# Two-layer trunk of attentions: the first head's loads on another queue, four projection tiles in another order, and another layout of on-chip memory for the second attention

## The chip, the cores and the metric

The kernel runs on one core of a Trainium2 chip. The metric is the device time of one execution in microseconds (us). One core has TensorE (matrix products, written to PSUM), VectorE, ScalarE and GpSimd, and SyncE, which here only starts DMAs. The engines run their own programs in order and wait for each other by semaphores. DMAs are started from the queues of SyncE, ScalarE and GpSimd and are carried out by 16 DMA engines that the core has for all of them. In the profile PE is TensorE, PEld its weight loads, DVE VectorE, ACT ScalarE, POOL GpSimd, SP SyncE; SPq, ACTq and POOLq are the starting of DMAs and other work of the sequencers.

## The reference

2048 tokens of width 1024 go through two layers, each `x <- LayerNorm(alpha * x + mixer(x))`. The mixer of layer 0 is a causal attention with forget gates (FoX), that of layer 1 a sparse attention (DSA): a small indexer selects 256 keys for each query, and only these count in the softmax. Both have 8 heads of 128 and a gate in front of the output weights.

```python
def _fox_mixer(x, w_in, b_f, w_out):
    q, k, v, f_logit, gate = _split(x @ w_in, [H * dh, H * dh, H * dh, H, D])
    cum = jnp.cumsum(jax.nn.log_sigmoid(f_logit + b_f), axis=1)
    ...
        s = einsum('bqhd,bshd->bhqs', q_b, k) * scale + c_b - cum_t
        s = where(kpos <= qpos, s, -inf)
        return einsum('bhqs,bshd->bqhd', softmax(s), v)
    ...
    return (silu(gate) * o) @ w_out

def _dsa_mixer(x, ..., w_in, kv_norm_g, w_uk, w_uv, w_out):
    q, ckv, kr, qi, ki, wi, gate = _split(x @ w_in, [H * dh, dc, dr, HI * di, di, HI, D])
    ...
        isc = einsum('bqhs,bqh->bqs', relu(einsum('bqhd,bsd->bqhs', qi_b, ki) * di ** -0.5), wi_b)
        isc = where(kpos <= qpos, isc, -inf)
        _, idx = lax.top_k(isc, k_sel)
        logits = einsum('bqhc,bqkc->bhqk', qf_b, kv_lat[idx]) * dh ** -0.5
        o_lat = einsum('bhqk,bqkc->bqhc', softmax(logits), sel[..., :dc])
    ...
    return (silu(gate) * o) @ w_out
```

## The kernel before, in words

Every operand is split into a high and a low half-precision part, and a product is three matmuls (`mm3`, lines 319 to 321: high by high, high by low, low by high). The split is a copy on ScalarE (line 328) and a subtraction (line 325) on GpSimd or VectorE.

The trunk runs one stage after the other: the projections of layer 0 (`fox_proj`), `attention(0)`, `out_proj(0)`, the projections of layer 1 (`dsa_jobs`, in three lists `first`, `second` and `rest`; the index scores and the selection run between them on VectorE and GpSimd and end in masks that GpSimd stores to DRAM, line 1647), `attention(1)`, `out_proj(1)`. Between stages K, V, q and the gates lie in DRAM tensors (`scr_k1`, `scr_kr` and `scr_kn`, `scr_v1`, `scr_v2`, `scr_q1`, ...).

`attention(layer)` goes through 8 heads and for each through four chunks of 512 queries, in the order `ORD[layer]`: (2, 3, 1, 0) in layer 0, (1, 0, 3, 2) in layer 1. For 128 queries `qk_tile` forms scores in PSUM, VectorE evacuates them with the mask or bias added and takes the minimum (line 1054, into a room PR), ScalarE takes the exponential and its sum (line 1068) and copies the high part (line 1076), GpSimd subtracts the low part (line 325, into PP), and a transposing DMA of SyncE turns the pair (line 1081) into one of the rooms PT, PU and PX, which are taken in turn (`TURNED`). In long chunks one row of each pair is turned on TensorE instead (line 1088). `pv_tile` multiplies with V. `gate` (line 1019 on) takes the reciprocal of the four sums and multiplies it into the gate; `pv_end` (line 1126) multiplies the result with it and stores it.

`load_kv` loads K and V of a head, `load_chunk` a chunk's q, `gate` the gate, `load_masks` the masks. All are issued by SyncE, save those of K and V of the first head (h = 0), which ScalarE issues. Loads of the next head are issued in between (`jobs`).

On-chip memory is a sequence of phases. `PHASE` says how many rooms of each tag a phase has, `SIZE` their bytes, `ORDER` the order in which they lie behind each other. Rooms of the next phase lie over those of the phase before, and an instruction that first writes a room waits for the last uses of all that lies under it. Phase 0 are the eight rooms `KV` of X1, the split output of layer 0, which the projections of layer 1 read; two of them (g = 0, 1) hold one chunk of 512 tokens. Phase 2 are the rooms of the second attention. Phase 5 are eight rooms P of the split output weights (`load_wo`, line 1153), taken by the pairs of `WOP`.

The instructions' order on each engine is made from the program by a scheduler that simulates a timeline; so a changed layout or queue moves others' places, too.

Of the kernel before, what the change touches and what calls it, by code (L numbers as in the profile page):

```python
# [15 lines left out]
F16 = mybir.dt.float16  # L16
# [33 lines left out]
         {"K": 4, "V": 2, "PT": 1, "PU": 1, "PX": 1, "PR": 4, "PP": 3, "M": 1, "N": 3}, {"P": 8},  # L50
         {"A": 3, "X": 15}, {"P": 8}, {})
ORDER = ((), ("N", "I", "PR", "PT", "pad1", "PU", "K", "PP", "V", "PX"),
         ("N", "M", "PX", "PR", "K", "V", "PP", "pad2", "PT", "PU"), ("pad3", "P"), ("A", "X"), (),
         ("st", "GB", "u", "GA", "GC", "spare"))
SIZE = {"K": 2048, "V": 4096, "PT": 8192, "PU": 8192, "PX": 8192, "PR": 4096, "PP": 4096, "I": 128, "N": 256,
        "M": 2432, "pad1": 3200, "pad2": 896, "pad3": 4096, "P": 4096, "A": 4096, "X": 4096, "st": 4096,
        "u": 3584, "spare": 4096, "GA": 8448, "GB": 10752, "GC": 7936}
TURNED = ("PT", "PU", "PX")

PS_BUFS = {"S": 3, "T": 2, "U": 2, "O": 1}  # L60
UTAGS = "SUSUS"
# [5 lines left out]
ORD = ((2, 3, 1, 0), (1, 0, 3, 2))  # L67
# [10 lines left out]
FTAGS = "STUSTUS"  # L78
SCAN = 2

WOP = (((0, 1), (2, 3), (4, 5), (6, 7)), ((3, 4), (2, 5), (6, 7), (1, 0)))
OGS = (0, 1, 2, 3), (0, 1, 1, 1)
OGE = 3
AHEAD = 13
# [135 lines left out]
def weave(main, side, start, end):  # L220

    at = []
    for k, (jobs, lo, hi) in enumerate(((main, 0.0, 1.0), (side, start, end))):
        total, done = sum(c for c, _ in jobs), 0.0
        for i, (c, job) in enumerate(jobs):
            at.append((lo + (hi - lo) * (done + 0.5 * c) / total, k, i, (c, job)))
            done += c
    return [x[3] for x in sorted(at, key=lambda x: x[:3])]


class Trunk:
# [736 lines left out]
    def load_kv(self, layer, h):  # L968
        nc = self.nc
        st = {"layer": layer}  # L970

        rooms = FIRSTK[layer] if h == 0 else (("K", 1024), ("K", 1024))
        st["k"] = []

        def key(s):
            while sum(n for _, n in rooms[:len(st["k"])]) < s + 1024:
                tag, n = rooms[len(st["k"])]
                a = sum(n for _, n in rooms[:len(st["k"])])
                to = self.t(tag, [128, 2, n], F16)
                for rows, name, r in ((slice(0, 32), "kr", 0), (slice(32, 128), "kn", h * 96)) if layer else (  # L980
                        (slice(0, 128), "k1", h * 128),):
                    (nc.sync if h else nc.scalar).dma_start(
                        to[rows], self.scr[name][r:r + rows.stop - rows.start, :, a:a + n])
                st["k"].append(to)
                for b in range(a, a + n, 512):
                    st[b] = to[:, :, b - a:b - a + 512]

        def value(s):
            if s == 0:
                st["v"] = self.t("V", [128, NT, 2, 128], F16)  # L990
            t = s // 128
            v = self.scr["v2" if layer else "v1"][h]
            (nc.sync if h else nc.scalar).dma_start(st["v"][:, t:t + 8], v[:, t:t + 8])

        return st, [partial(f, s) for f in (key, value) for s in range(0, S, 1024)]

    def load_chunk(self, layer, h, c):
        nc = self.nc
        cs = {"layer": layer, "h": h, "c": c, "l": self.sums[:, c, 4 * h:4 * h + 4], "halves": []}
        q, parts = self.pair(("SC" if layer else "RW") if (h, c) == (0, ORD[layer][0]) else "E")  # L1000
        nc.sync.dma_start(q, self.scr["q2" if layer else "q1"][c, h * 128:(h + 1) * 128])
        cs["q"] = parts
        if layer:
            return cs
        if self.rel[0] != h:
            self.rel = h, [self.t("W", [128, 1024]) for _ in range(2)]
            for a, t in enumerate(self.rel[1]):
                nc.sync.dma_start(t, self.scr["rel"][h:h + 1, a * 1024:a * 1024 + 1024].to_broadcast([128, 1024]))
        cs["rel"] = self.rel[1]
        return cs  # L1010
# [15 lines left out]
    def qk_tile(self, cs, j, i):  # L1026

        nc = self.nc
        c = cs["c"]
        qt = 4 * c + j  # L1030
# [29 lines left out]
        if i == 0:  # L1060
            yield "turn"
            self.half_i += 1
            turned = self.t(TURNED[self.half_i % len(TURNED)], [128, 4 * qt + 6, 128], F16)
            cs["halves"].append({"cs": cs, "half": j // 2, "T": turned})
        up = self.tiny(1)
        per, neg = (self.scale(x, cs["layer"]) for x in ("per", "neg"))
# [2 lines left out]
        turned = cs["halves"][-1]["T"]  # L1069
# [8 lines left out]
        if c >= MERGE:  # L1078
            turned = turned[:, 2 * qt:]
# [185 lines left out]
    def dsa_jobs(self):  # L1265

        nc, A = self.nc, self.A
# [141 lines left out]
        def jobs(order):  # L1409

            out = []
            for m, ch in order:
                if m not in kept:
                    kept[:] = kept[-KEPT:] + [m]
                    out.append((0.0, partial(load, m)))
                else:
                    kept[:] = [x for x in kept if x != m] + [m]
                out.append((5.2, partial(tile, m, ch)))
            return out
# [3 lines left out]
        def over(tiles, *chunks):  # L1423
            return [(m, ch) for ch in chunks for m in tiles]
# [10 lines left out]
                ups.append((0.0, partial(at, ch + 1)))  # L1435
            ups += [(0.7, partial(up_value, ch, j, s)) for j in range(4) for s in range(2)]
        rest = []
        for m in range(6, 22):
            rest += jobs(over((m,), 0, 1, 2, 3))
        return first, second, weave(weave(rest, ups, *UPS), [(1.0, up)], UPL, UPL)  # L1440


# [231 lines left out]
```

## Time and profile before

| | us |
|---|---|
| median of three runs | 2780.16 |
| the runs | 2783.97, 2780.16, 2772.90 |
| the profiled execution | 2781.16 |
| its span in the trace | 2779.4 |
| TensorE busy | 2517.8 (91%) |
| VectorE busy | 1888.0 (68%) |
| ScalarE busy | 1419.7 (51%) |
| GpSimd busy | 858.8 (31%) |

Mean granted clock of TensorE is 0.968 of its full speed. A busy share is a mean over all stages. The rows further down give a start in us from the start of the span, a duration, the engine, the line of the kernel, the operation with output and input tiles, and in brackets how long the engine was idle before and on what it waited.

### The profile page before, as it was taken

What the parts mean: (1) busy time and instruction counts of PE and PEld (TensorE: products, weight loads), DVE (VectorE), ACT (ScalarE), POOL (GpSimd) and SP (SyncE); (2) the same over time, 40 slices, a digit from 0 to 9 for tenths busy, and PEclk for the clock granted to TensorE, in tenths of its full rate; (3) what the DMA queues carried; (4) which work ended last, traced back from release to release, by engine and by line L of the source; (5) the groups of instructions that cost most, each with busy time, mean ns of one, the idle gap of its engine ahead of it and who ended that gap; (6) DMA issues with size and microseconds to landing.
All of it is one profiled execution on the core that took longest, in us unless ns stands there. A gap on an engine that the chain in (4) does not pass through costs nothing. (4 is left out here: it accounts for less than half of the span.)

```text
span 2779.4 us, 44011 instructions
## 1 busy us (share of the span) xinstructions
PE 2517.8 (91%) x15919; PEld 1636.5 (59%) x15919; DVE 1888.0 (68%) x4662; ACT 1419.7 (51%) x2283; POOL 858.8 (31%) x601
## 2 busy tenths in 40 slices
PE   8788989999988889889999989899978888888898
PEld 7688534444665666668845444444435666666687
DVE  4786655444766666667748899888955666666565
ACT  6464343322665666632326876774535666666310
POOL 3465643330333334442210211110013333333421
PEclk9899999999999999999999999999989999999999
DMA  7456645214988888864332432222678888777642
GB/s 263 162 187 204 211 126 173 76 65 151 210 204 171 184 188 181 165 198 141 124 97 61 123 90 64 69 75 82 197 217 190 192 178 184 173 163 151 183 144 88
DMA packets 583809, 424.20 MB, mean 153 GB/s; under 512 B 398048, under 2 KB 473584, under 8 KB 583584
## 3 DMA queue, kind: packets, MB, share of 16 engines
q1 hardware_dynamic: 580544, 412.78, 56.2%
q10 hardware_dynamic: 1984, 4.20, 0.5%
q0 software_dynamic: 1056, 4.36, 0.4%
q8 instruction: 125, 2.05, 0.3%
q14 instruction: 100, 0.82, 0.1%
HBM read 219.88 MB, written 109.08 MB: 118 GB/s over the span
## 5 line engine op out<-in xcount | busy, mean ns | idle before, releaser
L325 POOL TENSOR_TENSOR PP<-PR,PP 128x640 f16<-128x640 f32 (+3 forms) x192 | 375.8, 1971 | 697.0 <-ACT PP L1076 525.5
L1068 ACT ACTIVATE PR<-PR,ty,small 128x1152 f32<-128x1152 f32 (+15 forms) x256 | 330.1, 1290 | 249.5 <-DVE ty L1067 245.5
L325 POOL TENSOR_TENSOR W<-RW,W 128x512 fp32r<-128x512 f32 (+1 forms) x124 | 160.0, 1310 | 540.7 <-ACT W L328 469.5
L325 POOL TENSOR_TENSOR W<-A,W 128x512 f16<-128x512 f32 x114 | 136.5, 1218 | 228.8 <-ACT W L328 192.2
L320 PEld LDWEIGHTS <-W 128*128 128x128 f16 x1184 | 116.3, 98 | 147.1 <-issue 13.9
L321 PEld LDWEIGHTS <-W 128*128 128x128 f16 x1184 | 116.3, 98 | 137.9 <-issue 2.9
L319 PEld LDWEIGHTS <-W 128*128 128x128 f16 x1184 | 116.6, 98 | 137.3 <-issue 3.2
L1076 ACT ACTIVATE PP<-PR 128x640 f16<-128x640 f32 (+3 forms) x192 | 186.2, 980 | 18.0 <-DMA PX<-PP 7.5
L320 PEld LDWEIGHTS <-V 128*128 128x128 f16 x1152 | 117.0, 102 | 104.4 <-issue 81.8
L319 PE MATMUL T<-KV,W 128*128 128x512 f16 x464 | 176.9, 381 | 0.4 <-DVE E L1250 0.4
L320 PE MATMUL T<-KV,W 128*128 128x512 f16 x464 | 177.1, 382 | 0.0
L321 PE MATMUL T<-KV,W 128*128 128x512 f16 x464 | 176.9, 381 | 0.0
L328 ACT ACTIVATE W<-RW 128x512 fp32r<-128x512 f32 (+1 forms) x124 | 73.4, 629 | 181.6 <-PE U L320 93.6
L1054 DVE CUSTOM_DVE_ANT_0 PR<-S,W,ty 128x512 f32<-128x512 f32 (+3 forms) x209 | 138.8, 664 | 38.0 <-PE S L1049 18.1
L319 PEld LDWEIGHTS <-V 128*128 128x128 f16 x1152 | 116.9, 101 | 64.0 <-DMA PX<-PP 17.0
L319 PE MATMUL S<-K,E 128*128 128x512 f16 (+3 forms) x379 | 132.3, 349 | 11.5 <-DVE ty L1054 10.7
L378 ACT ACTIVATE SC<-E,tz 128x512 f16<-128x512 f32 (+1 forms) x78 | 50.8, 682 | 172.5 <-DVE E L540 102.6
L320 PE MATMUL S<-K,E 128*128 128x512 f16 (+3 forms) x379 | 132.3, 349 | 0.0
L321 PE MATMUL S<-K,E 128*128 128x512 f16 (+3 forms) x379 | 131.9, 348 | 0.0
L1480 ACT ACTIVATE SC<-S,small 128x512 f32<-128x512 f32 (+2 forms) x182 | 111.8, 635 | 35.4 <-DVE GC L1485 7.1
L321 PEld LDWEIGHTS <-V 128*128 128x128 f16 x1152 | 117.2, 102 | 20.1 <-issue 0.8
L1088 PE MATMUL T<-ident,PR 128*128 128x128 f32 x768 | 116.6, 277 | 3.4 <-DVE PU L325 1.7
(503 smaller groups left out, 7836.0 us busy)
## 6 DMA issues: line engine op xcount, KB each, us to landing
A<-in_fw SPq DMA_DIRECT2D x38, 512.0 KB
QS<-in_fw SPq DMA_DIRECT2D x32, 512.0 KB
E<-scr_g SPq DMA_DIRECT2D x64, 256.0 KB
scr_og<-SC SPq DMA_DIRECT2D x64, 256.0 KB
RW<-scr_og SPq DMA_DIRECT2D x64, 256.0 KB
E<-scr_q SPq DMA_DIRECT2D x62, 256.0 KB
V<-scr_v SPq DMA_DIRECT2D x28, 512.0 KB
scr_g<-E SPq DMA_DIRECT2D x48, 256.0 KB
```

Source lines behind the costliest of these rows:

```text
L319: first = mm(o, lh, rh, start=start, stop=False, skip_group_check=True)
L320: mm(o, lh, rl, start=False, stop=False, skip_group_check=True)
L321: mm(o, ll, rh, start=False, stop=stop, skip_group_check=True)
L325: eng.tensor_tensor(out=o, in0=a, in1=b, op=OP.subtract)
L328: self.nc.scalar.activation(hi, src, AF.Copy)
L378: nc.scalar.activation(out[0], src, AF.Copy, scale=scale)
L1054: nc.vector.tensor_tensor_reduce(out=row[:, lo:hi], in0=sc[:, lo - a:hi - a], in1=bias, op0=OP.add, op1=OP.min, scale=-1.0, scalar=3e38 if ...
L1068: nc.scalar.activation(row, row, AF.Exp, bias=up, scale=neg, accum_out=cs["l"][:, j:j + 1])
L1076: nc.scalar.activation(hi, row, AF.Copy)
L1088: nc.tensor.transpose(ps[:, (k - a) * 128:(k - a + 1) * 128], row[:, k * 128:(k + 1) * 128], self.ident)
L1480: nc.scalar.activation(t, ps[:, :w], AF.Relu, scale=self.scales[:, 24:25])
```

## The change

There are four parts. The loads of K and V of the first head, in both attentions, go from ScalarE's queue to GpSimd's, and the very first q from SyncE's to GpSimd's. The last four projection tiles of layer 1 (18 to 21, gate columns) are made chunk by chunk, in the order 2, 3, 1, 0, and no longer tile by tile. In the second attention the rooms lie in another order, and the turned rooms are taken in another rotation. The eight rooms of the output weights of layer 1 are paired otherwise.

```diff
 ORDER = ((), ("N", "I", "PR", "PT", "pad1", "PU", "K", "PP", "V", "PX"),
-         ("N", "M", "PX", "PR", "K", "V", "PP", "pad2", "PT", "PU"), ("pad3", "P"), ("A", "X"), (),
+         ("N", "PR", "K", "PX", "V", "PP", "PT", "PU", "M", "pad2"), ("pad3", "P"), ("A", "X"), (),
...
-TURNED = ("PT", "PU", "PX")
+TURNED = ("PT", "PU", "PX"), ("PU", "PX", "PT")
...
-WOP = (((0, 1), (2, 3), (4, 5), (6, 7)), ((3, 4), (2, 5), (6, 7), (1, 0)))
+WOP = (((0, 1), (2, 3), (4, 5), (6, 7)), ((4, 3), (0, 1), (2, 5), (7, 6)))
...
-                    (nc.sync if h else nc.scalar).dma_start(
+                    (nc.sync if h else nc.gpsimd).dma_start(
                         to[rows], self.scr[name][r:r + rows.stop - rows.start, :, a:a + n])
...
-            (nc.sync if h else nc.scalar).dma_start(st["v"][:, t:t + 8], v[:, t:t + 8])
+            (nc.sync if h else nc.gpsimd).dma_start(st["v"][:, t:t + 8], v[:, t:t + 8])
...
-        nc.sync.dma_start(q, self.scr["q2" if layer else "q1"][c, h * 128:(h + 1) * 128])
+        eng = nc.gpsimd if (h, c) == (0, ORD[layer][0]) else nc.sync
+        eng.dma_start(q, self.scr["q2" if layer else "q1"][c, h * 128:(h + 1) * 128])
...
-            turned = self.t(TURNED[self.half_i % len(TURNED)], [128, 4 * qt + 6, 128], F16)
+            turned = self.t(TURNED[cs["layer"]][self.half_i % 3], [128, 4 * qt + 6, 128], F16)
...
-        for m in range(6, 22):
+        for m in range(6, 18):
             rest += jobs(over((m,), 0, 1, 2, 3))
+        rest += jobs(over((18, 19, 20, 21), *ORD[0]))
```

**ScalarE at the start of the second attention.** Before, from the projection's last evacuation (line 371) to the second exponential. V and K are rooms of the first head (a name's number is that of the tile), `kr` and `kn` the two parts of K.

```order
1493 L371 ACTIVATE E_23336<-O_23311,small 128x512
1494 L1632 UNCONDITIONAL_BRANCH
1495 L993 DMA V_24193<-scr_v_69 128x2048
1496 L982 DMA K_24213<-scr_kr 32x2x1024
1497 L1068 ACT_TABLE_LOAD
1498 L1068 ACTIVATE PR_24173,N_24152<-PR_24173,ty_24188,small 128x640
1499 L982 DMA K_24213<-scr_kn 96x2x1024
1500 L993 DMA V_24193<-scr_v_69 128x2048
1501 L1076 ACTIVATE PP_24174<-PR_24173 128x5x128
1502 L1068 ACTIVATE PR_24173,N_24152<-PR_24173,ty_24207,small 128x768
```

With the change, the same stretch on to the fourth exponential:

```order
1486 L371 ACTIVATE E_23336<-O_23311,small 128x512
1487 L1634 UNCONDITIONAL_BRANCH
1488 L1069 ACT_TABLE_LOAD
1489 L1069 ACTIVATE PR_24173,N_24152<-PR_24173,ty_24188,small 128x640
1490 L1077 ACTIVATE PP_24174<-PR_24173 128x5x128
1491 L1069 ACTIVATE PR_24173,N_24152<-PR_24173,ty_24207,small 128x768
1492 L1077 ACTIVATE PP_24174<-PR_24173 128x6x128
1493 L1069 ACTIVATE PR_24218,N_24152<-PR_24218,ty_24233,small 128x896
1494 L1077 ACTIVATE PP_24219<-PR_24218 128x7x128
1495 L1069 ACTIVATE PR_24218,N_24152<-PR_24218,ty_24251,small 128x1024
```

The four DMAs are gone from ScalarE. On GpSimd they now stand between the last mask store and the first split of the attention:

```order
428 L1649 DMA scr_mask<-GA_19190 128x1920
429 L1649 DMA scr_mask<-GA_19190 128x2048
430 L993 DMA V_24193<-scr_v_69 128x2048
431 L982 DMA K_24213<-scr_kr 32x2x1024
432 L982 DMA K_24213<-scr_kn 96x2x1024
433 L993 DMA V_24193<-scr_v_69 128x2048
434 L325 TENSOR_TENSOR PP_24174<-PR_24173,PP_24174 128x5x128
435 L325 TENSOR_TENSOR PP_24174<-PR_24173,PP_24174 128x6x128
```

**SyncE at the same place.** Before: the loads of the next head (V_24348, K_24295, K_24310, K_25026), a query load E_24891, and behind them the first two transposes and the masks.

```order
882 L993 DMA V_24348<-scr_v_69 128x2048 x2
883 L982 DMA K_24295<-scr_kr 32x2x1024
884 L982 DMA K_24295<-scr_kn 96x2x1024
885 L982 DMA K_24310<-scr_kr 32x2x1024
886 L982 DMA K_24310<-scr_kn 96x2x1024
887 L982 DMA K_25026<-scr_kr 32x2x1024
888 L982 DMA K_25026<-scr_kn 96x2x1024
889 L1001 DMA E_24891<-scr_q_66 128x1024
890 L1081 DMA_TRANSPOSE PX_24187<-PP_24174 128x22x128
891 L1081 DMA_TRANSPOSE PT_24232<-PP_24219 128x30x128
892 L964 DMA M_24268<-scr_mask 128x1152
```

With the change:

```order
885 L993 DMA V_24348<-scr_v_69 128x2048
886 L982 DMA K_25026<-scr_kr 32x2x1024
887 L982 DMA K_25026<-scr_kn 96x2x1024
888 L1082 DMA_TRANSPOSE PT_24187<-PP_24174 128x22x128
889 L1082 DMA_TRANSPOSE PU_24232<-PP_24219 128x30x128
890 L964 DMA M_24268<-scr_mask 128x1152
...
897 L1082 DMA_TRANSPOSE PX_24289<-PP_24282 128x6x128
898 L1082 DMA_TRANSPOSE PT_24342<-PP_24316 128x14x128
899 L1128 DMA scr_og_78<-SC_24423 128x512
900 L1002 DMA E_24891<-scr_q_66 128x1024
```

The same loads of the next head stand ahead of the first transpose; the query load now comes behind the masks and two more transposes, and the turned rooms have other names.

**ScalarE's first splits of the output weights, with what each waits for.** Before, the first waits for a PE semaphore that the last PV matmul sets, since that matmul reads the room PX under P_30038:

```order
1875 L328 ACTIVATE P_30038<-E_30043 128x512 [waits DMAHW2_49,DMAHW4_49,DVE_49,PE_49]
1876 L328 ACTIVATE P_30038<-RW_30047 128x512
1877 L328 ACTIVATE P_30038<-E_30051 128x512 [waits DMAHW5_49]
1878 L328 ACTIVATE P_30038<-RW_30055 128x512
1879 L328 ACTIVATE P_30037<-E_30069 128x512 [waits DMAHW0_49]
```

With the change:

```order
1863 L328 ACTIVATE P_30039<-E_30043 128x512 [waits DMAHW4_49,Pool_49]
1864 L328 ACTIVATE P_30039<-RW_30047 128x512
1865 L328 ACTIVATE P_30039<-E_30051 128x512
1866 L328 ACTIVATE P_30039<-RW_30055 128x512
1867 L328 ACTIVATE P_30035<-E_30069 128x512 [waits DMAHW3_49,DMAHW2_49,PE_49]
```

The first room now waits for GpSimd's last split of the attention, which reads the room PR under it, and the second for the PV matmuls of the half in front of the last.

## Rows read from the trace of the kernel before

**Rows 1.** The page's busy times by engine (us, share of the span, instructions):

```profile
PE 2517.8 (91%) x15919; PEld 1636.5 (59%) x15919; DVE 1888.0 (68%) x4662; ACT 1419.7 (51%) x2283; POOL 858.8 (31%) x601
```

**Rows 2.** TensorE's instructions in order of time at the start of the second attention, those ahead of which it was idle longest (start, duration, line and tiles, in brackets the idle time and what ended it):

```profile
2075.39 0.58 PE L319 MATMUL S<-RW,E 128*128 128x512 f16 x1 [13.04 <-DVE ty L1054]
...
2087.25 0.37 PE L319 MATMUL O<-PX,V 128*128 128x256 f16 x1 [5.54 <-DMA PX<-PP]
...
2097.78 0.59 PE L319 MATMUL U<-K,E 128*128 128x512 f16 x1 [3.54 <-DVE ty L1054]
```

**Rows 3.** Busy time by stretch. Columns: the stretch, its length, then busy us of PE, PEld, DVE, ACT and POOL (with instructions), the granted TensorE clock, the DMA engines' busy share, GB/s:

```profile
2050.00:2056.00 6.00, 6.00 (x30) 2.77 (x29) 0.57 (x3) 1.22 (x2) 0.20 (x1) 1.00 0.88 283
2056.00:2062.00 6.00, 4.89 (x31) 2.54 (x29) 4.43 (x15) 0.15 (x1) 0.00 (x0) 1.00 0.76 181
2062.00:2068.00 6.00, 0.35 (x2) 0.07 (x1) 0.00 (x0) 2.29 (x3) 0.00 (x0) 0.87 1.03 353
2068.00:2078.00 10.00, 2.61 (x11) 1.73 (x11) 2.24 (x11) 7.87 (x15) 5.43 (x4) 0.50 1.00 223
2078.00:2090.00 12.00, 5.79 (x25) 2.88 (x23) 2.46 (x8) 2.94 (x7) 4.60 (x5) 0.64 1.15 211
2090.00:2098.00 8.00, 3.54 (x31) 2.85 (x30) 1.63 (x4) 0.00 (x0) 0.00 (x0) 0.93 0.93 294
...
2200.00:2300.00 100.00, 86.75 (x647) 62.48 (x646) 67.96 (x206) 64.55 (x97) 36.81 (x21) 0.98 0.89 195
```

**Rows 4.** VectorE in order of time at the same place: the first evacuation of the new attention, the fourth row minimum of the first chunk, and the reciprocal's first step:

```profile
2049.29 0.67 DVE L1054 CUSTOM_DVE_ANT_0 PR<-U,QS 128x512 f32<-128x512 f32 x1
...
2060.82 0.22 DVE L1067 TENSOR_SCALAR ty<-ty,small 128x1 f32<-128x1 f32 x1
2074.66 0.48 DVE L1019 TENSOR_SCALAR ty<-N,small 128x4 f32<-128x4 f32 x1 [13.62 <-ACT PR L1068]
```

**Rows 5.** ScalarE there: the table load, the first copy, the second and the fourth exponential:

```profile
2063.50 1.28 ACT L1068 ACT_TABLE_LOAD   x1 [7.35 <-DMA E<-scr_g]
...
2069.80 0.74 ACT L1076 ACTIVATE PP<-PR 128x640 f16<-128x640 f32 x1 [3.99 <-DMA V<-scr_v]
2070.45 1.01 ACT L1068 ACTIVATE PR<-PR,ty,small 128x768 f32<-128x768 f32 x1
...
2073.31 1.23 ACT L1068 ACTIVATE PR<-PR,ty,small 128x1024 f32<-128x1024 f32 x1
```

**Rows 6.** SyncE's queue there: first and last of the next head's loads, the first two transposes, the masks (the duration is that of the issue):

```profile
2060.28 2.59 SPq L993 DMA_DIRECT2D V<-scr_v  x2
...
2076.88 0.59 SPq L982 DMA_DIRECT2D K<-scr_kn  x1
...
2078.21 6.76 SPq L1081 DMA_TRANSPOSE PX<-PP  x1
2085.14 4.61 SPq L1081 DMA_TRANSPOSE PT<-PP  x1
2089.84 1.02 SPq L964 DMA_DIRECT2D M<-scr_mask  x2
```

**Rows 7.** GpSimd there: the last mask store (512 KB), and the second split of the first pair:

```profile
2049.67 0.54 POOL L1647 DMA_DIRECT2D scr_mask<-GA  x1 [0.17 <-issue]
...
2073.48 1.64 POOL L325 TENSOR_TENSOR PP<-PR,PP 128x768 f16<-128x768 f32 x1 [1.46 <-ACT PP L1076]
```

**Rows 8.** ScalarE's DMA issues between 2050 and 2100 (tiles, queue, count, size of one):

```profile
V<-scr_v ACTq DMA_DIRECT2D x2, 512.0 KB
...
K<-scr_kn ACTq DMA_DIRECT2D x1, 384.0 KB
```

**Rows 9.** The start of the first attention: a load of SyncE that waits for the room's last use, the first V load on ScalarE's queue, the key store, ScalarE behind it and TensorE behind that:

```profile
678.48 0.33 SPq L1008 DMA_DIRECT2D W<-scr_rel  x1
...
684.75 0.36 ACTq L993 DMA_DIRECT2D V<-scr_v  x1
...
685.87 0.52 SPq L579 DMA_DIRECT2D scr_k<-SC  x1
...
692.22 0.72 ACT L378 ACTIVATE SC<-E,tz 128x512 f16<-128x512 f32 x1 [5.98 <-DMA scr_k<-SC]
...
694.51 0.58 PE L319 MATMUL S<-QS,RW 128*128 128x512 f16 x1 [3.70 <-DVE ty L1054]
```

**Rows 10.** The projections of layer 0: a key load on ScalarE's queue, and GpSimd's splits:

```profile
466.11 0.63 ACTq L982 DMA_DIRECT2D QS<-scr_k  x1
...
466.23 2.27 POOL L325 TENSOR_TENSOR W<-A,W 128x512 f16<-128x512 f32 x2 [2.85 <-ACT W L328]
...
492.73 2.32 POOL L325 TENSOR_TENSOR W<-A,W 128x512 f16<-128x512 f32 x2 [17.03 <-ACT W L328]
```

**Rows 11.** The end of the second attention: TensorE's waits from 2587 on (total, times, longest), and the first splits of the output weights on ScalarE and GpSimd:

```profile
PE U L320 <- DVE P L325: 1.3, 3, 0.9
PE S L320 <- POOL P L325: 0.8, 2, 0.5
PE S L319 <- ACT P L328: 0.7, 1, 0.7
...
2587.66 0.63 ACT L328 ACTIVATE P<-E 128x512 fp32r<-128x512 f32 x1 [13.90 <-PE U L321]
...
2588.36 12.76 POOL L325 TENSOR_TENSOR P<-E,P 128x512 fp32r<-128x512 f32 x8 [11.76 <-ACT P L328]
```

## The prediction

> **What bounds the kernel now.** I read the page first: TensorE is busy for 2517.8 us of a span of 2779.4 [rows 1], so what can be won without taking matmuls away is some 260 us of its idle time, and a change is worth what it takes out of that. Then I looked for TensorE's idle time at the three places where the change puts something elsewhere: the starts of the two attentions and the end of the second one. The largest single wait of the three is at the start of the second attention. There TensorE stands still 13.04 us until 2075.39, then 5.54 us until 2087.25, then 3.54 us until 2097.78 [rows 2]. By stretches it works 0.35 of 6 us, 2.61 of 10, 5.79 of 12 and 3.54 of 8, while in the steady part, 2200 to 2300, it works 87 of 100 [rows 3].
>
> The wait of 13.04 us is traced back engine by engine. TensorE waits for a PSUM tile that VectorE evacuates (line 1054). VectorE has been idle 13.62 us in front of line 1019, which needs the sums of the first four exponentials [rows 4]. ScalarE ends its work on the projection at 2056.15, and then idles twice, 7.35 us in front of the table load and 3.99 us in front of the first copy of line 1076 [rows 5]. VectorE had the first four row minima ready by 2061.0 [rows 4], so what held ScalarE are the loads in its own program: the order above shows V, K, K and V in front of and between these instructions. They have to wait for earlier DMAs, and a queue is in order.
>
> The waits of 5.54 and 3.54 us are of another kind. The first transpose is issued on SyncE's queue only at 2078.21, behind the loads of the next head, which stand there from 2060.28 to 2076.88 in waits of their own; GpSimd had finished the pair it transposes at 2075.12. The masks follow at 2089.84 behind two transposes of 6.76 and 4.61 us [rows 6, 7]. In this stretch the DMA engines are busy all the time (shares 1.03, 1.00, 1.15), but with 353, 223 and 211 GB/s, and before it, 2050 to 2062, they have room (shares 0.88 and 0.76; 283 and 181 GB/s) [rows 3].
>
> **The change, part by part.** *Loads off ScalarE (second attention).* With the four loads gone from its program, ScalarE starts the table load at 2056.15. Its steps by their own durations (1.28 for the table; then about 1.0, 0.65, 1.0, 0.74, 1.1, 0.9 and 1.2 for the four exponentials with the three copies between them, as they follow each other from 2069.80 to 2074.54) end at about 2064.1 instead of 2074.54 [rows 5]. So line 1019, and with it TensorE's restart, can come 10.5 us earlier, at about 2064.9. GpSimd's pair would be done by about 2062.4 (copy done 2060.8, split 1.64) instead of 2075.12 [rows 7].
>
> How much of it survives the next two waits is decided on SyncE's queue and in the DMA engines. First head's V and K are 1.5 MB (two of 512 KB, one of 384 [rows 8], and 128 for the 32 rows of line 982's other part). GpSimd can issue them once its last mask store is out, at 2050.21 [rows 7], and then they use the room of 2050 to 2062: up to the 353 GB/s that the next stretch reaches, (353−283)×6 + (353−181)×6 = 1.45 MB. One query load of 256 KB, in front of the first transpose before, goes behind the masks. So up to 1.7 MB leave the stretch in front of the transpose; at the 223 GB/s of 2068 to 2078 that is 7.6 us. If the room is counted by shares instead (0.12×6 + 0.24×6 = 2.2 us, or 0.76 MB, and the 0.26 MB, at 353 GB/s), it is 2.9 us. **I take 7 us, bounds 2.9 and 10.5**: the slow stretch is the one from which the bytes go, and SyncE's loads there wait for landings, which come sooner. The masks follow the transposes on the same queue and shift with them. What comes earlier by then stays earlier: up to 2570 TensorE is busy 0.87 in the steady part and its DMA share is 0.89, below the start's.
>
> *The same for the first attention.* There ScalarE isn't held by its loads (its wait is 5.98 us for the landing of a key store that SyncE issued at 685.87, long after its own loads, and TensorE's wait of 3.70 us hangs on it) [rows 9]. The V loads, 1 MB, went out at 684.75; on GpSimd they wait for the projection's last use of the room alone, for which SyncE's load of 678.48 also waited [rows 9], so they go some 6 us earlier, ahead of that store instead of beside it. The key loads of the projection move to GpSimd between weight splits: the first is free when ScalarE issued it, 466.11, and GpSimd's next split started at 466.23 [rows 10], so it costs one issue, which I price by a mask store's (0.54 us) [rows 7]; it is hidden by the 17 us that GpSimd idles before the next unit. **I take 1 us of gain; bounds: 3.7 of gain, or 1 of loss** if V's bytes delay the store.
>
> *The projection tiles 18 to 21 by chunk.* The same matmuls into the same PSUM tiles; only their operands come in another order, and the weights are split well ahead of the tiles: nothing, either way.
>
> *The rooms.* At the start the first evacuation of the new attention, which ran at 2049.29 [rows 4], now lies over the chunk of X1 that the very last matmul of the projection reads; about 1.25 us of VectorE's work move to 2055.4. ScalarE is free only at 2056.15 and then loads its table until 2057.4, so this costs nothing; without that cover it would be 1.25 us. The order of PT, PU, PX only renames: each is still one of three in turn.
>
> At the end the first P room no longer lies under the tile that the last PV matmuls read, so the splits of the output weights start when GpSimd's last pair is done, about 2577, not at 2587.66 (ScalarE waited 13.90 us for TensorE there, GpSimd 11.76 us for ScalarE) [rows 11]. TensorE's waits for P from there on are 1.3 us (VectorE), 0.8 (GpSimd) and 0.7 (ScalarE), 2.8 in all [rows 11]. ScalarE's and GpSimd's go. VectorE's pieces stay behind the last gate product in its order, but they needn't wait for ScalarE's first split then, and have no GpSimd beside them, whose eight splits take 12.76 us there now. The reloads of the weights stay behind the last store on SyncE's queue. **I take 2 us, bounds 0 and 2.8.**
>
> **Sum.** 7 + 1 + 2 = 10 us. The profiled execution took 2781.16 us (span 2779.4), so about 2771; the median of the runs shown is 1 us lower, so 2770. The runs before spread over 11 us, 0.4%, and 0.5%, 13.9 us, is about what can be told from no change.
>
> **A rule that speaks against it.** The Trainium skill ("DMA: Bandwidth & Descriptors", section "Issuing engines are not separate DMA queues") says that DMAs started by ScalarE, SyncE and GpSimd run on the same 16 engines, and that another starting engine saves only the time of issuing. By that the 10.5 us would shrink to the bytes' bound of 2.9. The trace agrees in that the DMA share is full from 2062 on [rows 3]; it disagrees in that issuing was not a matter of fractions of a us here, since ScalarE was held 11.34 us in all [rows 5].
>
> **Rivals.**
> *A, the whole wait goes.* The transposes and the masks are late because SyncE's queue is in order and waits for landings, not for want of bandwidth. For it: 211 to 223 GB/s in a stretch that could carry 353. Then 10.5 + 2.8 + 1 to 3.7: 14 to 17 us, 2764. Against it: the loads of the next head are still in front.
> *B, bytes decide.* The transposes land only when everything in front of them has moved: 2.9 + 1 = 4 us, 2776. For it: the DMA shares of 1.0 to 1.15.
> *C, slower: GpSimd is held.* Its first split of the new attention now stands behind the four loads. A 512 KB mask store kept GpSimd 0.54 us [rows 7]. Should a load keep it 5.8 us or more, GpSimd would be free only at 2073.4 (2050.2 + 4×5.8), about when the second split of that pair started before, and every us beyond delays transposes and TensorE by one: at 8 us each, 9 us more, 2789. Nothing in the rows shows an issue of such length. The Trainium skill ("SBUF — State Buffer", section "SBUF: two separate sides") names a way to it: GpSimd writes the descriptors of its own DMAs and can't while VectorE holds the port that they share. By the rows VectorE works 0.57 us of 2050 to 2056 [rows 3], so this trace gives the rule little to bite on.
> *D, nothing happens:* the time at 2097.78 is set by the mask loads, which find the same queue as before; 2 to 3 us from the rest, 2777.
>
> **How the numbers follow.** The forecast (6 to 13.9 us of gain) 0.42; A 0.30; B and D together 0.21; C 0.07. A is faster by over 0.5% for nearly all of its weight, with little from the forecast's edge: 0.31. C is slower by over 0.5% in a bit over half of it: 0.04. The rest, 0.65, is within 0.5%. The range leaves out 0.05 to 0.1 at each side: 2761 (A with all bounds and the runs' spread) to 2780 (nothing gained). The forecast's own is 2766 to 2774.
>
> **What would show it.** Right: ScalarE's table load at about 2056, line 1019 of VectorE at about 2064, the first wait of TensorE below 4 us; the first transpose issued between 2066 and 2072; the mask wait over by about 2091; ScalarE's first P split near 2577. Each later step of the second attention would then lie some 7 us earlier, up to the end. Wrong: GpSimd's issues of over 2 us; the transposes still issued after 2076 (B, D); a first wait that is gone but a second one grown by the same (B); a key store of the first attention that lands after 692; a time under 2764 would say that the queue's order, not the bytes, was the bound (A).

## The result, and the profile after

The changed kernel takes 2762.73 us (median of 13 runs, 2752.11 to 2774.19), the kernel before 2778.91 in the runs beside it (13 runs, 2770.25 to 2789.67): a ratio of 0.9947, with a 95% interval of 0.993 to 0.9963. That is 10.3 to 19.5 us less, against the 10 that were forecast, and inside the range. Measured a second time (below) the ratio was 0.9978 (0.9957 to 0.9998). The profiled execution of the changed kernel, with a span of 2772.4 us, is the slowest of its 13 runs.

The page of the changed kernel answers to [rows 1]; the busy times differ little, and TensorE's is 11.8 us longer, not shorter, so the gain is idle time:

```profile
PE 2529.6 (91%) x15919; PEld 1644.5 (59%) x15919; DVE 1877.4 (68%) x4662; ACT 1419.7 (51%) x2283; POOL 864.1 (31%) x615
```

All times of this execution at the start of the second attention are 12.28 us earlier than in [rows 2 to 7], since so much had been gained before it, most of it by chance (see the end); to compare, add 12.28. TensorE's waits there, as in [rows 2]:

```profile
2050.07 0.28 PE L319 MATMUL U<-RW,E 128*128 128x256 f16 x1 [3.57 <-DMA E<-scr_q]
2053.11 0.61 PE L319 MATMUL U<-RW,E 128*128 128x512 f16 x1 [1.76 <-DMA E<-scr_q]
...
2071.09 0.37 PE L319 MATMUL O<-PT,V 128*128 128x256 f16 x1 [9.24 <-DMA PT<-PP]
...
2080.28 0.38 PE L319 MATMUL U<-K,E 128*128 128x512 f16 x1 [2.22 <-DVE ty L1055]
```

The wait of 13.04 us is gone. In its place stand 3.57 and 1.76 us for query loads, and the wait for the first turned tile has grown from 5.54 to 9.24. In the kernel before, one wait for a query load stands there:

```profile
2060.88 0.39 PE L319 MATMUL U<-RW,E 128*128 128x512 f16 x1 [1.11 <-DMA E<-scr_q]
```

ScalarE and VectorE (as in [rows 4, 5]) do what was forecast:

```profile
2043.89 1.28 ACT L1069 ACT_TABLE_LOAD   x1
...
2050.86 1.23 ACT L1069 ACTIVATE PR<-PR,ty,small 128x1024 f32<-128x1024 f32 x1
...
2052.22 0.73 DVE L1020 TENSOR_SCALAR ty<-N,small 128x4 f32<-128x4 f32 x1 [2.78 <-ACT PR L1069]
```

The table load has no wait in front of it, and VectorE's line (1019 before, 1020 now) starts at 2052.22, by the clock of before at 2064.5. GpSimd issues the four loads right behind the last mask store, in 0.54 to 0.67 us each:

```profile
2037.74 0.54 POOL L993 DMA_DIRECT2D V<-scr_v  x1 [0.27 <-issue]
2038.27 0.56 POOL L982 DMA_DIRECT2D K<-scr_kr  x1
2038.83 0.67 POOL L982 DMA_DIRECT2D K<-scr_kn  x1
2039.50 0.57 POOL L993 DMA_DIRECT2D V<-scr_v  x1
...
2048.93 1.64 POOL L325 TENSOR_TENSOR PP<-PR,PP 128x768 f16<-128x768 f32 x1 [0.48 <-ACT PP L1077]
```

The pair is split at 2050.57. But SyncE's queue (as in [rows 6]) issues the transpose 9.4 us later, and its issue alone takes 8.87 us:

```profile
2048.59 0.53 SPq L1002 DMA_DIRECT2D E<-scr_q  x1
2052.90 0.32 SPq L1018 DMA_DIRECT2D E<-scr_g  x1
2053.32 0.38 SPq L993 DMA_DIRECT2D V<-scr_v  x1
...
2058.01 0.59 SPq L982 DMA_DIRECT2D K<-scr_kn  x1
2059.97 8.87 SPq L1082 DMA_TRANSPOSE PT<-PP  x1
2068.95 4.53 SPq L1082 DMA_TRANSPOSE PU<-PP  x1
2073.59 1.00 SPq L964 DMA_DIRECT2D M<-scr_mask  x2
```

The loads in front of it stand there from 2053.32 to 2058.60, now nearly without waits among themselves; one wait of 3.7 us is ahead of them, which the profile puts down to the landing of a gate store. SyncE's waits for such stores there (total, times, longest), with the change and before:

```profile
SPq L1018 <- DMA scr_g<-E: 5.6, 2, 3.7
...
SPq L1017 <- DMA scr_g<-E: 0.7, 1, 0.7
```

At the start of the first attention (as in [rows 9]) and at the end of the second (as in [rows 11]):

```profile
664.66 1.08 POOL L993 DMA_DIRECT2D V<-scr_v  x2 [55.98 <-PE T L321]
...
676.99 0.52 SPq L579 DMA_DIRECT2D scr_k<-SC  x1
...
680.79 0.72 ACT L378 ACTIVATE SC<-E,tz 128x512 f16<-128x512 f32 x1 [3.42 <-DMA scr_k<-SC]
...
683.07 0.38 PE L319 MATMUL S<-QS,RW 128*128 128x512 f16 x1 [1.14 <-DVE ty L1055]
```

```profile
2570.55 0.62 ACT L328 ACTIVATE P<-E 128x512 fp32r<-128x512 f32 x1
...
2587.17 0.63 ACT L328 ACTIVATE P<-E 128x512 fp32r<-128x512 f32 x1 [11.33 <-DMA E<-in_do]
...
PE U L320 <- DVE P L325: 1.4, 3, 0.9
PE S L319 <- ACT W L328: 0.9, 1, 0.9
PE U L319 <- ACT P L328: 0.4, 1, 0.4
```

ScalarE's wait for the key store fell from 5.98 to 3.42 us, TensorE's behind it from 3.70 to 1.14. The first split of the output weights no longer waits for the last PV matmul; it runs 11.1 us ahead of the first matmul that needs it (2581.68).

### The profile page after: what moved, and what is told of

The parts are those of the page before. It is cut to its first block, busy times and chain, and to the rows that moved or that the text cites. A ratio compares the mean times of both kernels' runs of the same rounds, so it can differ in the third digit from the quotient of the medians.

```text
span 2772.4 us, 44038 instructions
## 1 busy us (share of the span) xinstructions
PE 2529.6 (91%) x15919; PEld 1644.5 (59%) x15919; DVE 1877.4 (68%) x4662; ACT 1419.7 (51%) x2283; POOL 864.1 (31%) x615
## 5 line engine op out<-in xcount | busy, mean ns | idle before, releaser
L320 PEld LDWEIGHTS <-V 128*128 128x128 f16 x1152 | 119.0, 103 | 102.4 <-issue 77.2
L319 PEld LDWEIGHTS <-V 128*128 128x128 f16 x1152 | 119.5, 104 | 70.7 <-DMA PT<-PP 14.3
L321 PEld LDWEIGHTS <-V 128*128 128x128 f16 x1152 | 119.6, 104 | 22.0 <-issue 0.6
```

What stands on the lines that cost most here:

```text
L319: first = mm(o, lh, rh, start=start, stop=False, skip_group_check=True)
L320: mm(o, lh, rl, start=False, stop=False, skip_group_check=True)
L321: mm(o, ll, rh, start=False, stop=stop, skip_group_check=True)
```

## The experiments

Since TensorE's instructions have the same places in all kernels here, a stage is measured from the start of one of its instructions to the start of another. "Start 1" is from the last waits of the layer 0 projections to the first scores behind the wait of [rows 9] (669.83 to 694.51 in the trace of before); "start 2" from the last matmuls of the layer 1 projections to the scores behind the mask wait (2053.71 to 2097.78 in the trace of before); "steady 2" from there to the last PV matmuls (2586.41); "hand-over" from there to the first matmul with the output weights (2588.34). The stages are from the trace of each kernel's one profiled execution, in us; a ratio is to the kernel before, in the runs beside it:

| kernel | ratio (95%) | start 1 | start 2 | steady 2 | hand-over |
|---|---|---|---|---|---|
| before | 1 | 24.68 | 44.07 | 488.6 | 1.92 |
| before2 | | 24.74 | 41.89 | 487.0 | 1.92 |
| changed | 0.9947 (0.993 to 0.9963) | 22.12 | 38.85 | 500.4 | 1.01 |
| again | 0.9978 (0.9957 to 0.9998) | 22.16 | 38.12 | 493.0 | 1.01 |
| queue | 0.9956 (0.9937 to 0.9975) | 21.94 | 37.45 | 489.5 | 1.97 |
| rooms | 1.0001 (0.9985 to 1.0017) | 24.51 | 43.28 | 488.5 | 1.01 |
| chunk | 0.9993 (0.9976 to 1.001) | 24.99 | 41.56 | 491.0 | 1.92 |
| queue1 | 0.9981 (0.9962 to 1.0) | 25.16 | 38.37 | 490.3 | 1.92 |
| sync | 0.9961 (0.9946 to 0.9976) | 21.58 | 41.78 | 486.7 | 1.92 |
| behind | 0.9937 (0.9917 to 0.9957) | 22.11 | 29.26 | 503.0 | 1.01 |
| behind_again | 0.9928 (0.991 to 0.9947) | 22.58 | 29.01 | 489.2 | 1.01 |
| behindq | 0.9958 (0.994 to 0.9976) | 21.98 | 29.08 | 495.4 | 1.92 |
| qchunk | 0.9964 (0.9948 to 0.9981) | 22.33 | 37.75 | 493.3 | 1.92 |
| qrooms | 0.9937 (0.9923 to 0.9951) | 22.26 | 38.75 | 490.0 | 1.01 |

**again, and before2.** The two kernels unchanged.

> The changed kernel as it is, once more, for a second profiled execution. In the first one TensorE was 17.5 us ahead of the kernel before at the first long scores of the second attention, and only 6.7 us ahead at its end. If the steady part of the second attention is slower by the change (its rooms, its queues), it takes about 501 us again from the first long scores to the first matmul with the output weights, against 490.6 before. If that was a matter of the one execution, it lies near 490. Likewise at the forget gates of the first attention: a 128x128 operation of VectorE (line 890) took 8.06 us before and 0.99 in the changed kernel; if that is chance, it can be long here too. Time: 0.994 to 0.996 of before either way.

> The kernel before once more, for a second profiled execution. If the 8.06 us of VectorE's 128x128 operation at line 890 were chance, it is about 1 to 3 us here, and everything behind it lies some 6 us earlier; from the last matmul of the layer 1 projections to the first long scores of the second attention it takes about 44 us again, from there to the output weights about 490.

Starts and hand-over repeat within some 2 us. The steady part doesn't: 500.4 and 493.0 us for the same program. The operation at line 890 took 3.26 us in the second execution of the changed kernel and 1.04 in the second of the kernel before, whose span was 2764.8, against the 2779.4 of [rows 1]: 14.6 us between two executions of one program, of which TensorE's wait behind this operation is 6.2.

**queue.** The loads alone:

```diff
-                    (nc.sync if h else nc.scalar).dma_start(
+                    (nc.sync if h else nc.gpsimd).dma_start(
-            (nc.sync if h else nc.scalar).dma_start(st["v"][:, t:t + 8], v[:, t:t + 8])
+            (nc.sync if h else nc.gpsimd).dma_start(st["v"][:, t:t + 8], v[:, t:t + 8])
-        nc.sync.dma_start(q, ...)
+        eng = nc.gpsimd if (h, c) == (0, ORD[layer][0]) else nc.sync
+        eng.dma_start(q, ...)
```

> The kernel before with one part of the change: first head's K, V and the first q of both attentions on GpSimd's queue. Theory one (the prediction's): this is where the gain comes from, 8 us, ratio 0.997, with ScalarE's table load right behind its last evacuation and TensorE's wait of 13.04 us below 4 us. Theory two: the queue alone gains little (0.999 to 1.0), since the transposes and masks behind the next head's loads stay as late as they were, and the gain measured for the whole change comes from the rooms.

Theory one: 0.9956, and both starts as in the changed kernel. This part is the gain.

**rooms.** `ORDER`, `TURNED` and `WOP` as in the change, nothing else.

> The kernel before with one part of the change: the order of the second attention's rooms, the rotation of the turned rooms and the pairing of the output weights' rooms. Theory one: only the end of the second attention moves, 2 us, ratio 0.999, ScalarE's first output weight split near 2577 by the clock of before. Theory two: 6 us or more (0.998 and below), and the gain is seen at the start or in the steady part of the second attention.

No difference in time that can be told, against 2 us expected; the interval reaches 4 us less. The hand-over is 0.9 us shorter, and the starts and the steady part are as before.

**chunk.** Only `rest` made chunk by chunk.

> The kernel before with one part of the change: the projection tiles 18 to 21 chunk by chunk. Theory one: nothing, ratio 0.999 to 1.001, no wait of TensorE on a weight there. Theory two: 0.998 or below, if the rooms of X1 that come free earlier let the second attention's first loads go earlier even with the old layout.

Nothing that can be told, as expected.

**queue1.** The loads on GpSimd in layer 1 alone, `(nc.sync if h else (nc.gpsimd if layer else nc.scalar))`.

> The kernel before with the loads of the second attention alone on GpSimd (K, V of the first head and the first q); the first attention's stay on ScalarE. Theory one: the second attention's start takes about 38 us from the projections' last matmul to the first long scores instead of 44, the first attention's start keeps its wait of 3.7 us; 6 us gained, ratio 0.998. Theory two: if most of the gain of both was in the first attention, 0.999 to 1.0.

Start 2 is 38.37 us and start 1 stays at 25.16; 5.3 us less by the ratio, with an interval that just reaches none. So the two starts are independent, and by these stages the second attention's is the larger.

**sync.** K and V of the first head on SyncE's queue like all others (the first q stays there too):

```diff
-                    (nc.sync if h else nc.scalar).dma_start(
+                    nc.sync.dma_start(
-            (nc.sync if h else nc.scalar).dma_start(st["v"][:, t:t + 8], v[:, t:t + 8])
+            nc.sync.dma_start(st["v"][:, t:t + 8], v[:, t:t + 8])
```

> The kernel before with K and V of the first head on SyncE's queue, as those of all other heads, in both attentions; nothing is issued by ScalarE or GpSimd. Theory one (ScalarE's program was held, and GpSimd's early issue gives room): ScalarE is free as with GpSimd's queue, and TensorE's first wait at the second attention shrinks to 3 us; but the 1.5 MB now stand in one line ahead of the transposes, which are issued about as late as before, so that the second wait takes the first one's place: 0 to 3 us gained there. Theory two (only ScalarE's program counted): the same 5 to 6 us at the second attention as with GpSimd's queue.

At start 2 theory one: 41.78 us, nothing gained against 41.6 to 44.1, though ScalarE was as free as with GpSimd's queue. The first of SyncE's loads, and TensorE's waits over that start, from the projections' end on (total, times, longest):

```profile
2042.51 0.38 SPq L993 DMA_DIRECT2D V<-scr_v  x1
...
PE O L319 <- DMA PX<-PP: 10.8, 1, 10.8
PE U L319 <- DMA K<-scr_kn: 3.5, 1, 3.5
PE S L319 <- DVE ty L1054: 2.8, 1, 2.8
```

The first wait shrank from 13.04 to 2.8 us, and most of it came back: 10.8 for the first turned tile instead of 5.54, and 3.5 for a key. Freeing ScalarE alone is worth little or nothing there. On GpSimd's queue the four loads were issued 3.7 to 1.9 us ahead of the mark at the projections' last matmuls (2041.43 in the changed kernel), on SyncE's not before 6.6 us behind it (2042.51, with the mark at 2035.93). That this earlier time makes the difference, and not the second queue as such, is likely, but no run tells the two apart. In the first attention, on the other hand, leaving ScalarE is enough (21.58). Over the whole kernel 0.9961 was measured, 11 us, of which these stages show 3 to 4; the rest is not explained.

**behind, and once more as behind_again.** The changed kernel, with the second head's K and V behind the first two transposes and the masks in SyncE's order (`follow` sets an order without a wait):

```diff
                         self.follow(load, self.turns[-1], "what comes first is loaded first")
+                    self.mask_load = load
...
-                    (nc.sync if h else nc.gpsimd).dma_start(
+                    load = (nc.sync if h else nc.gpsimd).dma_start(
                         to[rows], ...)
+                    if layer and h == 1:
+                        self.follow(load, self.mask_load, "behind the masks")
...
-            (nc.sync if h else nc.gpsimd).dma_start(st["v"][:, t:t + 8], v[:, t:t + 8])
+            load = (nc.sync if h else nc.gpsimd).dma_start(st["v"][:, t:t + 8], v[:, t:t + 8])
+            if layer and h == 1:
+                self.follow(load, self.mask_load, "behind the masks")
```

> The changed kernel, with the next head's K and V loads at the start of the second attention put behind the first transposes and the masks on SyncE's queue (order alone, no wait). Theory one: what is left of the gap, 9.24 us of TensorE for the first transposed tile, is the wait of that transpose behind 2.5 MB of loads; the transpose is issued some 7 us earlier relative to the end of the projection and the wait falls to 3 us or less; 4 to 6 us less than the changed kernel, ratio to the kernel before 0.993. Theory two: a transpose takes 9 us by itself, or the masks behind it become the bound: the wait stays, ratio as for the changed kernel, 0.995 to 0.998.

> The changed kernel with the second head's loads behind the first transposes and masks, once more, for a second profiled execution: about 29 us again from the projections' last matmul to the first long scores. Theory one: 495 us or more again in the steady part. Theory two: 488 to 491, if the 503 us were chance. Time: 0.992 to 0.995 of before either way.

The split of the first pair, the queue of SyncE and TensorE at that place (the projections' last matmuls start at 2035.20):

```profile
2042.71 1.64 POOL L325 TENSOR_TENSOR PP<-PR,PP 128x768 f16<-128x768 f32 x1 [0.49 <-ACT PP L1082]
...
2045.84 0.32 SPq L1023 DMA_DIRECT2D E<-scr_g  x1
2046.33 4.14 SPq L1087 DMA_TRANSPOSE PT<-PP  x1
...
2051.20 4.96 SPq L1087 DMA_TRANSPOSE PU<-PP  x1
2056.27 0.99 SPq L964 DMA_DIRECT2D M<-scr_mask  x2
```

```profile
2052.48 0.27 PE L319 MATMUL O<-PT,V 128*128 128x256 f16 x1 [0.29 <-DMA PT<-PP]
...
2058.76 0.37 PE L319 MATMUL O<-PU,V 128*128 128x256 f16 x1 [3.23 <-DMA PU<-PP]
...
2064.46 0.38 PE L319 MATMUL U<-K,E 128*128 128x512 f16 x1 [1.54 <-DVE ty L1060]
```

Theory one, at this place by more than it said: the wait for the first turned tile is 0.29 us instead of 9.24 (that for the second is 3.2 instead of 0.7), the transpose is issued 2.0 us after its pair is split instead of 9.4 and lands at most 6.2 us after its issue instead of 11.1, and start 2 is 29 us. 0.9937 and 0.9928 are, with the 0.9937 of qrooms, the lowest ratios here, 17 to 20 us less than before. But the intervals overlap with that of the changed kernel, the two weren't timed side by side, and behindq, which adds this order to *queue*, comes out no lower than *queue* (0.9958 and 0.9956). So 9 us are shown for this start, and not for the whole kernel.

**behindq, qchunk, qrooms.** These were to find where the long steady part came from: behindq is *behind* without the rooms and the projection order, qchunk is the change without its rooms, qrooms the change without its projection order.

> The kernel before with two things: the first head's loads and the first q on GpSimd, and the second head's K and V loads of the second attention behind the first transposes and masks; rooms and projection order as before. Theory one (what is given back in the steady part belongs to the other rooms, since the three executions with them took 493 to 503 us from the first long scores to the end and those without 487 to 491): about 29 us from the projections' last matmul to the first long scores, then 488 to 491, and a ratio of 0.990 to 0.992. Theory two (an earlier start is given back by TensorE's clock or by the loads that now come later, whatever the rooms): 29 us, then 497 us or more, ratio 0.993 to 0.996.

> The changed kernel without its rooms: first head's loads on GpSimd and the projection tiles 18 to 21 by chunk. Theory one: as the loads alone, 488 to 491 us in the steady part, ratio 0.995 to 0.996. Theory two: 493 or more, if the order of the projections is what changes the steady part.

> The changed kernel without its order of the projection tiles: first head's loads on GpSimd and the new rooms. Theory one: 493 to 503 us in the steady part of the second attention as in the changed kernel, ratio 0.996 to 0.998. Theory two: 488 to 491 and 0.995, if the longer steady part was chance or needs the order of the projections as well.

behindq has theory two's ratio, and 495.4 us between the two; qchunk and qrooms came out nearer to their second theories, 493.3 and 490.0 us. With the rooms the steady part was 488.5, 490.0 and 489.2 us as well as 493.0, 500.4 and 503.0, without them 487 to 495, so the rooms alone don't make it long. Nor does the projection order alone: *behind_again* has it with 489.2, behindq lacks it with 495.4. The five executions whose start 2 took over 41 us have 487 to 491, mean 488.3; the six of 37 to 39 us 489 to 500, mean 492.7; the three of 29 us 489 to 503, mean 495.9. So some of what an earlier start gains may be given back in the steady part, but *behind* alone gave 503.0 and 489.2, and single executions can't settle it.

What the rows do show is where such differences lie. Columns as in [rows 3]; the steady part of the second attention in the kernel before and in the changed one, then the first attention in the two executions of *behind*:

```profile
2097.78:2586.41 488.63, 427.09 (x3088) 306.99 (x3088) 319.41 (x966) 303.19 (x442) 180.62 (x90) 0.94 0.79 172
2080.28:2580.66 500.38, 436.96 (x3088) 313.16 (x3088) 318.58 (x966) 308.47 (x452) 189.17 (x97) 0.92 0.79 169
...
683.76:1189.74 505.98, 446.28 (x3348) 325.73 (x3348) 335.84 (x1005) 318.89 (x481) 204.33 (x108) 0.98 0.84 193
679.92:1197.97 518.05, 455.12 (x3348) 329.52 (x3348) 335.79 (x1006) 319.25 (x481) 204.43 (x108) 0.96 0.85 189
```

Of the 11.8 us more in the steady part 9.9 are TensorE's own busy time for as many matmuls, at a mean granted clock of 0.92 instead of 0.94. Two executions of one program differ by 12.1 us in the first attention, 8.8 of them busy time, at 0.98 and 0.96. So a stage of 500 us in a single execution can differ by 12 us without any change. What lowers the clock in one execution and not in the other is not shown.

It stays open whether the change makes the steady part longer, and also why qrooms came out at 0.9937 (0.9923 to 0.9951) where its stages show no more than those of the changed kernel, and below qchunk (0.9964, 0.9948 to 0.9981), which was timed beside it. If the projection order costs something together with the moved loads, these runs can't tell how.

## Why the prediction was right

The direction, the places and the range were right. That the sum of 10 us came near the result has luck in it: it lies just outside the first interval (10.3 to 19.5 us) and inside the second (0.6 to 12), and it was put together from terms that were each off, by stages 4.3 + 2.7 + 1.7 = 8.7 us against 7 + 1 + 2.

- *Second attention's start, 7 us, measured 4.3* (means of the table: 42.5 us in the five kernels without these loads on GpSimd, 38.2 in the six with them and nothing else). The mechanism was right step by step: ScalarE's table load with no wait, VectorE's line at 2064.5 where 2064 was said, the pair split at 2050.57 (2062.85 by the clock of before, where 2062.4 was said). Right too was that SyncE's queue and the bytes decide how much of 10.5 us passes. The step that was mis-sized is the room of 2050 to 2062: 1.45 MB by GB/s, 0.76 by shares. The count by shares was nearer. The rows fit that the loads take what they get there from the query loads: TensorE waited 5.3 us for two of those, against 1.1 us for one before (1.5 in *sync*, where nothing is loaded so early), and SyncE 3.7 us for a gate store in the same stretch, against 0.7. The first transpose came at 2072.25 by the clock of before, just behind the 2066 to 2072 that were said, and the mask wait was over at 2092.56, where 2091 was said.
- *First attention's start, 1 us, measured 2.7.* I had kept the loss in the bounds because V's bytes might delay the key store. They came far enough ahead of it: 664.66 against the store's 676.99. ScalarE went on 3.8 us after that store was issued, against 6.35 in [rows 9], where V goes out 1.1 us ahead of it; in *sync*, where V comes behind the store, it took 3.25. So the rows fit that V costs the store time only when they go side by side.
- *End, 2 us, measured 1.7* up to the kernel's last matmul, 0.9 of it at the hand-over (from the last PV matmuls to that last one 182.97 to 185.30 us, mean 183.5, in the eight executions without the new rooms, and 181.13 to 182.34, mean 181.8, in the six with them). ScalarE's first split came at 2576.3 by the clock of before, where 2577 was said. The 0.7 us of [rows 11] for ScalarE went (0.4 came elsewhere), and GpSimd's 0.8. VectorE's wait stayed (1.4), and ScalarE, done early with what it had, waited 11.33 us for a reload that stands behind the last store on SyncE's queue, so that the next operand (W, 0.9 us) became late. I named that order, but took nothing off for it.
- *The projection order, nothing; a load's issue on GpSimd, 0.54 us*: right (0.54 to 0.67). VectorE's evacuation behind the last matmul cost nothing that the rows show.
- *Rivals.* A said that the queue's order and not the bytes holds the transposes. For the change that didn't come: the second wait grew, as B said. *behind* shows that A had a reason, too: once nothing of the next head is in front, 9 us more of start 2 go. But that takes away the order and the bytes at once: the transpose is issued 7.4 us sooner after its pair, and lands 5.0 us sooner after its issue. B's price for this place, 2.9 us, was nearer than mine. C, GpSimd held by its issues, didn't happen, nor did D, as start 2 became shorter. My sign that a time under 2764 us would speak for A was wrong: 2762.73 came with the longer second wait in the trace, so a time alone couldn't tell A from the rest.
- *"Each later step some 7 us earlier, up to the end"* was not seen in that execution: 17.5 us ahead at the first long scores, 5.8 at the last PV matmuls. Between them lies the steady part, longer here mostly by TensorE's busy time at a lower clock.

The rule of the Trainium skill that was weighed ("DMA: Bandwidth & Descriptors", section "Issuing engines are not separate DMA queues"), that another starting engine saves only the time of issuing, was nearer to the runs at the second attention than I allowed: with the loads on SyncE's queue, where ScalarE is free, start 2 gained little or nothing. What the move to GpSimd gives there goes with an earlier time of issue.

The stages give 8.7 us, the two comparisons 14.7 (10.3 to 19.5) and 6.1 (0.6 to 12). The changed kernel's median is nearly the same in both, 2762.73 and 2764.89 us. That of the kernel before is 2778.91 in the first, and 2773.07, 2773.54 and 2772.79 in the three later ones. So what the first comparison has beyond the stages lies mostly in its runs of the kernel before, and not all of the 16 us between its medians should be put down to the change.

## What to carry to other kernels

A DMA that an engine issues can hold that engine's program while it waits for earlier DMAs (ScalarE for 11.3 us here), so look at what stands behind it. But before taking it away, follow the next thing that the same result waits for, as freeing ScalarE alone only moved the wait. A load is worth moving to a queue on which it can go earlier, into a stretch where the DMA engines have room; here that gave 4.3 us, less than the room by GB/s promised. And what belongs to the next unit should not stand ahead of a transpose or mask that the present one needs: putting it behind took 9 us more off this start, though over the whole kernel that gain is not clearly shown.

## What the runs showed of the hardware

A 128x128 operation of VectorE (line 890) took 0.4 to 8.1 us in different executions. In the kernel before:

```profile
386.31 8.06 DVE L890 TENSOR_SCALAR E<-E,ty 128x128 f32<-128x128 f32 x1 [7.35 <-DMA ty<-scr_cum]
...
389.68 1.28 POOL L325 TENSOR_TENSOR A<-A 128x512 f32<-128x512 f32 x1
390.90 3.40 POOL L325 TENSOR_TENSOR W<-A,W 128x512 f16<-128x512 f32 x3
```

It ends at 394.37, 0.07 us after GpSimd's row of splits, which has no gap from 385.12 to 394.30. In the second execution of the changed kernel it took 3.26 us, to 388.76, and GpSimd's row ended at 388.69:

```profile
385.50 3.26 DVE L890 TENSOR_SCALAR E<-E,ty 128x128 f32<-128x128 f32 x1 [7.11 <-DMA ty<-scr_cum]
...
387.42 1.27 POOL L325 TENSOR_TENSOR A<-A 128x512 f32<-128x512 f32 x1
389.23 3.39 POOL L325 TENSOR_TENSOR W<-A,W 128x512 f16<-128x512 f32 x3 [0.54 <-ACT W L328]
```

In both, VectorE's operation got through when GpSimd first paused. TensorE's next matmul waited 6.23 us in the first case, and not at all in the changed kernel's first execution, where the operation took 0.99 us; this is most of the 8.9 us by which the stretch up to start 1 is longer there (669.83 and 660.96 us). The Trainium skill ("SBUF — State Buffer", section "SBUF: two separate sides") says that the two engines share a port that one holds for a whole instruction; these rows agree, and show VectorE left out over seven instructions in a row. In all 14 executions the operation ended some 0.1 us after the end of an instruction of GpSimd. In ten of them this was already the one that was running when the operation began, or the next, with no pause behind it (0.4 to 1.5 us); in four the operation was left out up to a pause (3.3 to 8.1 us). What decides between the two is not shown.

A transpose of 22 blocks took 4.14 us to issue with none of the next head's loads in front of it (4.2 and 4.3 in the other two such kernels' executions) and 8.87 us right behind these 2.5 MB (6.8 to 9.4 in the ten others).
